# Modulation pieces of four k-tiles by 512 columns, and a ring of their own for the chunks that are not split

## The chip, the cores and the metric

The kernel runs on one core of a Trainium2 chip. The metric is the device time of one execution in microseconds (us); three runs of the kernel before are shown, and one execution was also profiled.

## What is computed

One layer of a hybrid diffusion backbone over 256 latent tokens and 256 context tokens with 2048 channels, in fp32. Cut to what matters here:

```python
mod_x = jnp.split((silu(c) @ w_ada + b_ada)[:, None, :], N_MOD, axis=-1)         # w_ada: 2048 x 12288, N_MOD = 6
mod_c = jnp.split((silu(c_ctx) @ w_ada + b_ada)[None, None, :], N_MOD, axis=-1)
hc = modulate(rmsnorm(ctx, norm1_w), mod_c[0], mod_c[1])    # modulate(h, shift, scale) = h * (1 + scale) + shift
hx = modulate(rmsnorm(x, norm1_w), mod_x[0], mod_x[1])
core_c, ctx_states = branch_core(hc, 1, p, None)            # h @ w_in, then the mixers
core_x, _ = branch_core(hx, rows, p, ctx_states)
x = x + mod_x[2] * branch_out(core_x, p)
hx2 = modulate(rmsnorm(x, norm2_w), mod_x[3], mod_x[4])
x = x + mod_x[5] * peer(hx2, ...)
```

The change is about the first two lines: two rows of activations (`c` and `c_ctx`) times the 96 MB matrix `w_ada`. Its first third (shift and scale of the first norm) is needed before anything else can be multiplied; the rest is needed late, from `mod_x[2]` on.

## The kernel before

**The stream of weights.** Weights reach the core as chunks of 128 x 1024 fp32 (512 KB). `Stream` (from line 33) holds a `plan`, the list of chunks in the order of their use. `ahead()` (line 58) issues loads through SP's queue up to `loads` = 7 chunks ahead of use (`_load`, line 39) and splits up to `splits` = 3 chunks ahead (`_split`, line 47). A split writes `hi`, the chunk rounded to fp32r, on ACT (line 52), and `lo = chunk - hi` on DVE (line 53); three fp32r matmuls (hi by hi, hi by lo, lo by hi) then stand for one fp32 product. The loaded chunks have a ring `raw` of 7 - 3 = 4 buffers, `hi` and `lo` of 4 each. Each `get()` takes the next chunk and calls `ahead()`.

**Modulation chunks are not split.** They stand in the same plan with a flag `False`, wait in the same raw ring (in the start two of three go to five more buffers, `raw0`, of the side pool `xp`), and are multiplied in fp32, which is two passes on PE. `ada_piece` (line 248) uses one chunk: four matmuls whose stationary side is `cS` (silu of `c` and `c_ctx`, two columns of 32 in use, line 244), each on a group of 32 columns of the array, side by side (`tile_position`), 256 columns each.

**Blocks.** `w_ada`'s first third (`w_ada0`) is 16 blocks of 4 chunks; a piece has four k-tiles by 256 columns. The rest (`w_ada1`, called `ride`) is 16 blocks of 8 chunks; a piece has two k-tiles by two 256-column halves. At the end of a block `ada_out` (line 256) copies the PSUM half bank `ad` to `adasb` on ACT (line 259), and two steps later PE transposes it in two pieces (line 264); DVE adds the four groups up (line 270) and adds `b_ada` (line 271) into `mods`.

**The start.** `START` (lines 139 to 150) is a list of steps, run by the loop in lines 369 to 402, and also sets the first part of the plan. In each of its first eight rounds come four chunks of block 8 + c (scale) and four of block c (shift), a step `h` (`h_pair`, line 296: two k-tiles of the normed and modulated input, `Hhi` and `Hlo`), and two each of the steps `v` (`v_part`, matmuls in lines 322 to 324) and `ld` (lines 393 to 395), from round 5 on also one chunk of k. Each piece also drives the generator `norm1` (line 279): per step four squares on ACT (line 284), three adds on DVE, a matmul with ones (line 287); then Ln and Exp (lines 289, 290), then eight multiplications of `xc` by the norm (line 293), two k-tiles each. The first `ahead()` stands at line 207, ahead of the constants (`ident` and on) and of all this.

**The units.** After the start come the projections as units (k, q, r, v, xs, ...); `mm3` (line 309, matmuls 314 to 316) does eight k-tiles of one chunk. `tick` (line 342) is called once per unit chunk, runs the waiting generators a step (`step`, line 333), and after every `RIDE` = 2 chunks lets `ride_piece` (line 349) do one modulation piece. 120 of the 128 ride that way, and `FILL` = 8 are done in a run near the second norm (loop near line 1122), from buffers of their own.

Of the kernel before, what the change touches and what calls it, by code (L numbers as in the profile page):

```python
# [10 lines left out]
F32 = mybir.dt.float32  # L11
F32R = mybir.dt.float32r
U32 = mybir.dt.uint32
# [15 lines left out]
class Stream:  # L29
# [3 lines left out]
    def __init__(self, nc, pool, loads, splits):  # L33
        self.nc, self.pool, self.loads, self.splits = nc, pool, loads, splits
        self.plan, self.raw, self.done = [], {}, {}
        self.cur = self.nd = self.ns = 0
        self.limit = self.side = None

    def _load(self, i):
# [4 lines left out]
        self.nc.sync.dma_start(t, self.plan[i][0])  # L44
        self.raw[i] = t

    def _split(self, i):
        t = self.raw.pop(i)
        if self.plan[i][1]:
            hi = self.pool.tile([P, 1024], F32R, name="hi", tag="hi", bufs=self.splits + 1)  # L50
            lo = self.pool.tile([P, 1024], F32R, name="lo", tag="lo", bufs=self.splits + 1)
            self.nc.scalar.activation(hi, t, AF.Copy)  # L52
            self.nc.vector.tensor_sub(lo, t, hi.bitcast(F32))  # L53
            self.done[i] = (hi, lo)
        else:
            self.done[i] = t
# [25 lines left out]
def hybrid_block_kernel(ctx, tc, A, out):  # L82
# [8 lines left out]
    st = Stream(nc, streams, 7, 3)  # L91
# [13 lines left out]
    def f_chunks(arr, f):  # L105
        return [(arr[f, h], True) for h in range(arr.shape[1])]
# [5 lines left out]
    RIDE, FILL = 2, 8  # L112
# [10 lines left out]
    def v_chunks(hd, q):  # L123
        return [(A["w_v"][hd, 2 * q + i], True) for i in range(2)]

    def unit_chunks(u):
        k, a, b = u
        first, n = {"k": (K0 + 2 * a + b, 1), "q": (Q0 + 2 * a, 2), "r": (R0 + 4 * a, 4), "xs": (X0 + 4 * a + b, 1),
                    "B": (B0 + a, 1), "C": (C0 + a, 1), "z": (Z0 + 4 * a + 2 * b, 2), "gl": (G0 + 2 * a, 2),
                    "v": (0, 0)}[k]  # L130
        if k == "v":
            return sum((v_chunks(a, q) for q in range(4)), [])
        if k == "k" and a < 2:
            return [(W[first, 1], True)]
        return sum((f_chunks(W, first + i) for i in range(n)), [])
# [16 lines left out]
    plan = []  # L152
    for k, a, b in START:
        if k == "ada":
            plan.append((A["w_ada0"][a, b], False))
        elif k == "v" and b == 0:
            plan.append((A["w_v"][0, a], True))
        elif k == "ld" and b == 0 and a % 2 == 0:
            plan.append((A["w_ld"][a // 2], True))
        elif k == "k":  # L160
            plan.append((W[K0 + a, 0], True))
    st.limit = len(plan)
    ride = [(A["w_ada1"][b, i], False) for b in range(16) for i in range(8)]
    nt = 0
    for u in units:
        for c in unit_chunks(u):
            plan.append(c)
            nt += 1
            if nt % RIDE == 0 and len(ride) > FILL:
                plan.append(ride.pop(0))  # L170
    assert len(ride) == FILL
# [6 lines left out]
    last_ada = ride  # L178
    QORD = [(j, e, h) for h in range(2) for j in range(2) for e in range(2)]
    QORD += [(j, e, h) for j in range(2, 8) for e in range(2) for h in range(2)]  # L180
    plan += [(A["w_q"][2 * j + e, h], True) for j, e, h in QORD]
    NB = 32
    for b in range(NB + BACK):
        for i in range(4):
            if b < NB:
                plan += f_chunks(A["u"], 4 * b + i)
            if b >= BACK:
                plan += [(A["v"][b - BACK, 2 * i + j], True) for j in range(2)]
# [3 lines left out]
    xpool = ctx.enter_context(tc.tile_pool(name="hpool", bufs=1))  # L192
# [13 lines left out]
    st.side = (xp, 5)  # L206
    st.ahead()
# [6 lines left out]
    ones512 = consts.tile([P, 256], F32, name="ones512")  # L214
    nc.vector.memset(ones512, 1.0)
# [7 lines left out]
    selF = consts.tile([P, 2, P], U32, name="selF")  # L223
    selB = consts.tile([P, 2, P], U32, name="selB")
    for n in range(2):
        nc.vector.tensor_scalar(selF[:, n], jp, 0.0, None, op0=OP.is_ge)
        nc.vector.tensor_scalar(selB[:, n], jp, 0.0, None, op0=OP.is_le)
# [20 lines left out]
    def ada_piece(i, ps, halves, raw=None):  # L248

        raw = (st.get() if raw is None else raw).rearrange("p (g n) -> p g n", g=4)  # L250
        nk = 4 // halves
        for g in range(4):
            mm_(ps[32 * g:32 * g + 32, :], cS[:, nk * i + g // halves, :], raw[:, g, :], start=i == 0, stop=i == KT // nk - 1,  # L253
                tile_position=(0, 32 * g), skip_group_check=True)

    def ada_out(b, ps, halves):

        sb = xpool.tile([P, 256], F32, name="adasb", tag="adasb", bufs=2)
        nc.scalar.activation(sb, ps, AF.Copy)
        yield  # L260
        yield
        p2 = scbank((P, 2, P))
        for t in range(2):
            nc.tensor.transpose(p2[:, t], sb[:, t * P:(t + 1) * P], ident)
        yield
        p2 = p2.rearrange("p t (j h m) -> p h t m j", h=halves, m=32)
        for h in range(halves):
            n = 2 * (halves * b + h)
            dst = mods[:, :, n:n + 2]
            nc.vector.tensor_reduce(dst.rearrange("p m t -> p t m"), p2[:, h, :, 0:2, :], axis=AX.X, op=OP.add)  # L270
            nc.vector.tensor_add(dst, dst, b_ada[:, None, n:n + 2].to_broadcast([P, 2, 2]))
        ended.add(("ada", b))
        yield
# [57 lines left out]
    ride_n, ride_ps = 0, None  # L331
# [17 lines left out]
    def ride_piece(raw=None):  # L349
        nonlocal ride_n, ride_ps  # L350
        b, i = divmod(ride_n, 8)
        if i == 0:
            ride_ps = adb[:, b % 2]
        ada_piece(i, ride_ps, 2, raw)
        if i == 7:
            bg.insert(0, ada_out(8 + b, ride_ps, 2))
        ride_n += 1
# [6 lines left out]
    adb = psum.tile([P, 2, 256], F32, name="ad")  # L364
    pv0 = [mmbank() for _ in range(4)]
    n1 = norm1()
    plr = pdt = None
# [36 lines left out]
    st.ahead()  # L404
    SZ = {"s1": 256, "s2": 512, "s4": 1024}
# [6 lines left out]

    lrS = wk.tile([P, 512], F32R, name="lrS")
# [29 lines left out]
    def decay(hd):  # L443
# [10 lines left out]
        def one(d, k):  # L454
# [12 lines left out]
            for n in range(2):  # L467
                s = slice(n * P, n * P + P) if d == 0 else slice(n * P + P - 1, n * P - 1 if n else None, -1)
                nc.vector.tensor_tensor_scan(B[:, k, s], ones512[:, :P], mn[:, s], 0.0, op0=OP.mult, op1=OP.add)
# [4 lines left out]
            nc.vector.tensor_tensor_scan(B[:, k, o], ones512[:, :255], mn[:, s], 0.0, op0=OP.mult, op1=OP.add)  # L474
# [152 lines left out]
    def dt_stage(pd):  # L627
# [26 lines left out]
        for c in range(4):  # L654
            s = slice(c * P, c * P + P)
            r = slice(c * P + P - 1, c * P - 1 if c else None, -1)
            nc.vector.tensor_tensor_scan(cum[rows[0], s], ones512[rows[0], :P], dA[rows[0], s], 0.0, op0=OP.mult, op1=OP.add)
            nc.vector.tensor_tensor_scan(cum[rows[1], r], ones512[rows[1], :P], dA[rows[1], r], 0.0, op0=OP.mult, op1=OP.add)
# [419 lines left out]
    def wo_load(i):  # L1078

        if i < 8:  # L1080
            nc.gpsimd.dma_start(x1[:, 2 * i:2 * i + 2], A["xc"][:, 2 * i:2 * i + 2, 0:256])
            if i < FILL:
                fill.append(x1p.tile([P, 1024], F32, name="fill", tag="fill", bufs=FILL))
                nc.gpsimd.dma_start(fill[-1], last_ada[i][0])
# [37 lines left out]
    for t in fill:  # L1122
        ride_piece(t)
# [183 lines left out]

    pq = {}
# [174 lines left out]
def _layouts(I):  # L1483
# [6 lines left out]
    L["w_ada0"] = f(w[:, :2 * D].reshape(4, 4, P, 16, 256).transpose(3, 0, 2, 1, 4)).reshape(16, 4, P, 1024)  # L1490
# [53 lines left out]
```

## Time and profile before

| | |
|---|---|
| time, median of three runs | 3682.08 us (3681.17 to 3683.45) |
| time of the profiled execution | 3680.64 us |
| its span on the core | 3678.8 us |
| granted TensorE clock, mean | 0.996 |
| PE matmuls, busy | 3619.1 us (98%), 24799 instructions |
| PE weight loads, busy | 3194.6 us (87%) |
| DVE, ACT, POOL busy | 61%, 45%, 10% |
| DMA | 715.51 MB, mean 194 GB/s |

The span is the time from the first to the last recorded instruction; 1.8 us of the execution lie around it. Busy times are of one profiled execution. Matmuls are pipelined and their ends are modelled, so that the distance between starts of matmuls tells more than their durations. A time in a timeline is counted from the start of the span. "Idle before" is the time in which an engine did nothing before an instruction, with the releaser, what ended it.

### The profile page before, as it was taken

How to read it: one execution, taken by the hardware profiler on the slowest of the kernel's cores; microseconds unless marked ns; L12 is line 12 of the kernel's file. 1: busy time of each engine (PE TensorE's matmuls, PEld its weight loads, DVE VectorE, ACT ScalarE, POOL GpSimd, SP SyncE). 2: the span in 40 equal slices, each digit the busy share in tenths (PEclk: the TensorE clock that was granted, in tenths of full speed). 3: DMA queues.
4: the chain of work that ended last, by engine and by line, in shares of the span. 5: the costliest groups of instructions: out<-in, count | busy, mean ns of one | idle time of the engine just before them, and what ended most of it. 6: DMA issues, size and time to landing. Idle time of an engine off the chain costs nothing.

```text
span 3678.8 us, 60850 instructions
## 1 busy us (share of the span) xinstructions
PE 3619.1 (98%) x24799; PEld 3194.6 (87%) x24799; DVE 2227.3 (61%) x3405; ACT 1669.3 (45%) x2248; POOL 370.1 (10%) x424
## 2 busy tenths in 40 slices
PE   6999999999999999999999999999999999999998
PEld 3688888888888888899999999999999999998886
DVE  4364443565566566656555788785555555556777
ACT  3244443344544455555444445554444444444444
POOL 0000000000000000011002006362000000000004
PEclk9999999999999999999999999999999999999999
DMA  8564444546555564467657556677665666666764
GB/s 341 214 177 142 151 166 164 188 152 199 192 172 164 185 204 144 135 206 266 195 189 258 176 179 197 200 200 228 197 198 196 199 197 198 196 199 202 244 227 141
DMA packets 196873, 715.51 MB, mean 194 GB/s; under 512 B 22769, under 2 KB 22913, under 8 KB 196081
## 3 DMA queue, kind: packets, MB, share of 16 engines
q1 hardware_dynamic: 171648, 625.03, 50.9%
q0 software_dynamic: 24944, 86.59, 8.5%
q8 instruction: 195, 3.19, 0.4%
q14 instruction: 86, 0.70, 0.1%
HBM read 679.93 MB, written 31.60 MB: 193 GB/s over the span
## 4 chain that ended last, share of the span: by engine, by line
PE 94%; DVE 2%; DMA 1%; ACT 1%; issue 1%; SPq 0%; POOL 0%; DVEq 0%; ACTq 0%; POOLq 0%
PE mm L314 20%; PE mm L315 20%; PE mm L316 20%; PE mm L1459 6%; PE mm L1460 6%; PE mm L1461 6%; PE ad L253 2%; PE mm L322 2%; PE sc L838 2%; PE mm L323 2%; PE mm L324 2%; PE sc L1267 2%; DVE lo L53 1%; PE sc L579 1%; PE sc L771 1%
## 5 line engine op out<-in xcount | busy, mean ns | idle before, releaser
L53 DVE TENSOR_TENSOR lo<-raw,hi 128x1024 fp32r<-128x1024 f32 x996 | 1235.1, 1247 | 1044.2 <-ACT hi L52 1040.4
L52 ACT ACTIVATE hi<-raw 128x1024 fp32r<-128x1024 f32 x996 | 1048.2, 1058 | 1248.8 <-PE mm L315 549.6
L314 PE MATMUL mm<-Hhi,hi 128*128 128x256 f32 (+1 forms) x2272 | 741.9, 327 | 3.7 <-ACT hi L52 3.1
L316 PE MATMUL mm<-Hhi,lo 128*128 128x256 f32 (+1 forms) x2272 | 723.0, 318 | 2.5 <-DVE lo L53 2.5
L315 PE MATMUL mm<-Hlo,hi 128*128 128x256 f32 (+1 forms) x2272 | 722.1, 318 | 0.0
L314 PE MATMUL mm<-h2hi,hi 128*128 128x256 f32 x2304 | 656.9, 285 | 3.3 <-ACT h2hi L1135 3.3
L315 PE MATMUL mm<-h2lo,hi 128*128 128x256 f32 x2304 | 652.4, 283 | 0.2
L316 PE MATMUL mm<-h2hi,lo 128*128 128x256 f32 x2304 | 651.8, 283 | 0.0
L314 PEld LDWEIGHTS mm<-Hhi,hi 128*128 128x128 f32 x2272 | 433.0, 191 | 82.3 <-issue 45.8
L316 PEld LDWEIGHTS mm<-Hhi,lo 128*128 128x128 f32 x2272 | 433.5, 191 | 33.0 <-DVE lo L53 3.1
L315 PEld LDWEIGHTS mm<-Hlo,hi 128*128 128x128 f32 x2272 | 433.7, 191 | 28.0 <-issue 0.5
L314 PEld LDWEIGHTS mm<-h2hi,hi 128*128 128x128 f32 x2304 | 441.6, 192 | 7.0 <-ACT h2hi L1135 3.7
L315 PEld LDWEIGHTS mm<-h2lo,hi 128*128 128x128 f32 x2304 | 441.9, 192 | 3.9 <-DVE h2lo L1138 0.7
L316 PEld LDWEIGHTS mm<-h2hi,lo 128*128 128x128 f32 x2304 | 441.6, 192 | 0.0
L1460 PE MATMUL mm<-lo,ph 128*128 128x512 f32 x1024 | 405.6, 396 | 4.5 <-DVE lo L53 4.5
L1459 PE MATMUL mm<-hi,ph 128*128 128x512 f32 x1024 | 406.3, 397 | 0.0
L1461 PE MATMUL mm<-hi,pl 128*128 128x512 f32 x1024 | 404.9, 395 | 0.0
L1460 PEld LDWEIGHTS mm<-lo,ph 128*128 128x128 f32 x1024 | 192.7, 188 | 48.6 <-DVE lo L53 6.0
L1461 PEld LDWEIGHTS mm<-hi,pl 128*128 128x128 f32 x1024 | 192.7, 188 | 46.6
L1459 PEld LDWEIGHTS mm<-hi,ph 128*128 128x128 f32 x1024 | 193.0, 188 | 43.1
L698 DVE SCALAR_TENSOR_TENSOR s<-mm,convw,s 128x189 f32<-128x189 f32 (+2 forms) x384 | 160.1, 427 | 111.5 <-ACT s L690 107.5
L316 PE MATMUL mm<-yh,lo 128*128 128x256 f32 x768 | 217.5, 283 | 1.3 <-DVE lo L53 1.3
(328 smaller groups left out, 4518.1 us busy)
## 6 DMA issues: line engine op xcount, KB each, us to landing
raw<-in_w_f_dram SPq DMA_DIRECT2D x288, 512.0 KB, 3.7
raw<-in_u_dram SPq DMA_DIRECT2D x256, 512.0 KB, 3.5
raw<-in_v_dram SPq DMA_DIRECT2D x256, 512.0 KB, 4.2
raw<-in_w_ada_dram SPq DMA_DIRECT2D x184, 512.0 KB, 4.3
raw<-in_w_so_dram SPq DMA_DIRECT2D x64, 512.0 KB, 3.4
raw<-in_w_v_dram SPq DMA_DIRECT2D x32, 512.0 KB, 3.9
s<-cum_d POOLq DMA_DIRECT2D x64, 256.0 KB, 6.6
raw<-in_w_ga_dram SPq DMA_DIRECT2D x32, 512.0 KB, 4.8
```

What stands on the lines that cost most here:

```text
L52: self.nc.scalar.activation(hi, t, AF.Copy)
L53: self.nc.vector.tensor_sub(lo, t, hi.bitcast(F32))
L253: mm_(ps[32 * g:32 * g + 32, :], cS[:, nk * i + g // halves, :], raw[:, g, :], start=i == 0, stop=i == KT // nk - 1, tile_position=(0, 32 ...
L314: mm_(ps, Whi[:, j, :], hi[:, k, tok], start=start and j == 0, stop=False)
L315: mm_(ps, Whi[:, j, :], lo[:, k, tok], start=False, stop=False)
L316: mm_(ps, Wlo[:, j, :], hi[:, k, tok], start=False, stop=stop and j == n - 1)
L322: mm_(pv[tb], Hhi[:, k, tok], Whi[:, j, :], start=k == 0, stop=False)
L323: mm_(pv[tb], Hhi[:, k, tok], Wlo[:, j, :], start=False, stop=False)
L698: nc.vector.scalar_tensor_tensor(dst, xi[:, r0 + dr:r1 + dr, c0 + dc:c1 + dc], w[:, t:t + 1], dst, op0=OP.mult, op1=OP.add)
L1459: mm_(ps[t, i], ghi, Whi, start=j == 0 and k == 0, stop=False)
L1460: mm_(ps[t, i], ghi, Wlo, start=False, stop=False)
L1461: mm_(ps[t, i], glo, Whi, start=False, stop=j == 1 and k == 1)
```

## The change

- The unsplit chunks leave the plan. They are a list of their own, `rides`, loaded in pairs by `board()` and taken by `alight()`. They have a ring `ride` of two buffers; in the start the five `raw0` of the side pool come on top, so that up to six chunks are aboard there (7 buffers), and two later. `board()` is called before the first `ahead()`, after each piece of the start, and in the units on the tick after a piece (`ticks % RIDE == 1`).
- The stream has 6 loads instead of 7, so its raw ring has 3 buffers. Its plan holds split chunks alone.
- A piece takes two chunks: four k-tiles by 512 columns, one k-tile per column group, into a whole bank `adb`. `w_ada0` is now 8 blocks of 4 pieces (each block has shift and scale of two k-tiles; its layout on the host follows), `w_ada1` 16 blocks of 4 pieces. In the start a piece stands on each odd step; `norm1` is driven two steps by each. `RIDE` is 4, `FILL` is 4.
- `ada_out` copies 512 columns into a buffer shared with others (`s4`, `s2`, `o2`), and instead of two transposes and a sum on DVE does four fp32 matmuls: stationary is a 128x128 part of the copy, moving is `sel2`, 128 x 2, which picks the two rows and adds the four groups. One addition on DVE with `b_ada` follows.
- `ones512`, `selF` and `selB` are replaced by broadcast views of `ones`, `maskF` and `maskB`.

```diff
     def _load(self, i):
-        if self.side and not self.plan[i][1] and i % 3:
-            t = self.side[0].tile([P, 1024], F32, name="raw0", tag="raw0", bufs=self.side[1])
-        else:
-            t = self.pool.tile([P, 1024], F32, name="raw", tag="raw", bufs=self.loads - self.splits)
...
+    def board(self):
+        while self.nr < len(self.rides) and len(self.aboard) + 2 <= 2 + (self.side[1] if self.side else 0):
+            for _ in range(2):
+                if self.side and self.nr % 7 > 1:
+                    t = self.side[0].tile([P, 1024], F32, name="raw0", tag="raw0", bufs=self.side[1])
+                else:
+                    t = self.pool.tile([P, 1024], F32, name="ride", tag="ride", bufs=2)
+                self.nc.sync.dma_start(t, self.rides[self.nr])
+                self.aboard.append(t)
+                self.nr += 1
...
-    st = Stream(nc, streams, 7, 3)
+    st = Stream(nc, streams, 6, 3)
...
-    RIDE, FILL = 2, 8
+    RIDE, FILL = 4, 4
...
-            if c < 8:
-                START.append(("ada", (8 + c, c)[i // 4], i % 4))
+            if c < 8 and i % 2:
+                START.append(("ada", c, i // 2))
...
     st.side = (xp, 5)
+    st.board()
     st.ahead()
...
+    sel2 = consts.tile([P, 2], F32, name="sel2")
+    nc.vector.tensor_reduce(sel2, ident.rearrange("p (j m) -> p m j", m=32)[:, 0:2, :], axis=AX.X, op=OP.add)
...
-        for g in range(4):
-            mm_(ps[32 * g:32 * g + 32, :], cS[:, nk * i + g // halves, :], raw[:, g, :], ...
+        raws = [r.rearrange("p (k n) -> p k n", k=2) for r in (raws or st.alight())]
+        for g in range(4):
+            mm_(adb[32 * g:32 * g + 32, :], cS[:, 4 * i + g, :], raws[g // 2][:, g % 2, :], ...
...
+    def ada_out(b):
+        sb = ada_sb()
+        nc.scalar.activation(sb, adb, AF.Copy)
+        yield
+        yield
+        p2 = scbank((P, 4, 2))
+        for t in range(4):
+            mm_(p2[:, t], sb[:, t * P:(t + 1) * P], sel2, start=True, stop=True)
+        yield
...
-        if riding and ticks % RIDE == 0 and ride_n < 128 - FILL:
+        if riding and ticks % RIDE == 0 and ride_n < 64 - FILL:
             ride_piece()
+        elif ticks % RIDE == 1:
+            st.board()
...
         if k == "ada":
-            if b == 0:
-                ps = adb[:, a // 8]
-            ada_piece(b, ps, 1)
+            ada_piece(b)
+            if st.nr < start_rides:
+                st.board()
             if b == 3:
-                bg.append(ada_out(a, ps, 1))
+                bg.append(ada_out(a))
+            next(n1, None)
             next(n1, None)
```

The lines move with it. In the changed kernel the split is in lines 49 (`hi`) and 50 (`lo`), a load of the stream in line 42, of `board` in line 61, the Silu of `cS` in line 247 and the squares of `norm1` in line 290.

The order of ACT's instructions at the head of the program, before (`sq` are the squares of `norm1`):

```order
L244 ACT_TABLE_LOAD [waits DMASW0_49]
L244 ACTIVATE cS<-cc 128x16x2 [waits DVE_49]
L245 ACT_TABLE_LOAD
L284 ACTIVATE sq_168<-xc 128x512 [waits DMAHW0_49]
L284 ACTIVATE sq_169<-xc 128x512
```

and in the changed kernel:

```order
L49 ACT_TABLE_LOAD
L49 ACTIVATE hi<-raw 128x1024 [waits DMAHW2_49]
L49 ACTIVATE hi<-raw 128x1024 [waits DMAHW3_49]
L49 ACTIVATE hi<-raw 128x1024 [waits DMAHW4_49]
L247 ACT_TABLE_LOAD [waits DMASW0_49]
L247 ACTIVATE cS<-cc 128x16x2 [waits DVE_49]
L248 ACT_TABLE_LOAD
L290 ACTIVATE sq_183<-xc 128x512 [waits DMAHW0_49]
```

Three splits, each behind its own transfer, now stand ahead of `cS` and of the first square; DVE's three `lo` (line 50) stand in the same way ahead of `ident` and the other constants.

The order of SP's loads in the changed kernel, in the block of the start that holds the second chunk of w_v (`ride` and numbered `raw` are modulation chunks; `raw<-in_w_ld` is a split chunk of the stream's ring):

```order
L61 DMA ride<-in_w_ada_dram 128x1024 [waits DMAHW0_49,PE_49]
L61 DMA ride<-in_w_ada_dram 128x1024 [waits DMAHW1_49,PE_49]
L42 DMA raw<-in_w_ld_dram 128x1024 [waits DMAHW2_49,DVE_49]
L61 DMA raw_429<-in_w_ada_dram 128x1024 [waits DMAHW3_49,PE_49]
L61 DMA raw_431<-in_w_ada_dram 128x1024 [waits DMAHW4_49,PE_49]
L61 DMA raw_461<-in_w_ada_dram 128x1024 [waits DMAHW5_49,PE_49]
```

The load of w_ld waits for DVE, which has to read an older chunk out of that ring, and the modulation chunks behind it wait only for PE; with one queue they go in this order.

## Rows read from the trace of the kernel before

**Rows 1.** The page, part 4: the chain that ended last, by engine.

```profile
PE 94%; DVE 2%; DMA 1%; ACT 1%; issue 1%; SPq 0%; POOL 0%; DVEq 0%; ACTq 0%; POOLq 0%
```

**Rows 2.** Timeline, PE: start us, us, engine line op out<-in xcount [idle before].

```profile
46.74 0.79 PE L322 MATMUL mm<-hi,Hhi 128*128 128x512 f32 x1
...
62.34 0.64 PE L253 MATMUL ad<-raw,cS 128*32 128x256 f32 x8 [0.56 <-ACT adasb L259]
...
74.13 1.93 PE L253 MATMUL ad<-raw,cS 128*32 128x256 f32 x32
76.63 0.64 PE L253 MATMUL ad<-raw,cS 128*32 128x256 f32 x8 [0.56 <-ACT adasb L259]
...
175.55 0.50 PE L314 MATMUL mm<-Hhi,hi 128*128 128x512 f32 x1 [0.50 <-ACT s L440]
```

**Rows 3.** Timeline of all engines, 602.4 to 604.2 us.

```profile
602.57 0.28 PE L316 MATMUL mm<-Hhi,lo 128*128 128x256 f32 x1
...
602.77 0.16 PEld L253 LDWEIGHTS ad<-raw,cS 128*32 128x32 f32 x8
602.78 0.64 PE L253 MATMUL ad<-raw,cS 128*32 128x256 f32 x8
...
603.34 0.19 PEld L314 LDWEIGHTS mm<-Hhi,hi 128*128 128x128 f32 x1 [0.41 <-issue]
603.35 0.50 PE L314 MATMUL mm<-Hhi,hi 128*128 128x512 f32 x1
603.45 0.19 PEld L315 LDWEIGHTS mm<-Hlo,hi 128*128 128x128 f32 x1
...
603.68 0.39 PE L315 MATMUL mm<-Hlo,hi 128*128 128x512 f32 x1
```

**Rows 4.** The chain that ended last, in order of time: start us, us, line.

```profile
757.78 3.43 PE sc L771 x8
```

**Rows 5.** Timeline, PE, 262.4 to 263.8 us.

```profile
262.87 0.28 PE L316 MATMUL mm<-Hhi,lo 128*128 128x256 f32 x1
262.99 0.38 PE L264 MATMUL sc<-ident,adasb 128*128 128x128 f32 x2
...
263.33 0.28 PE L315 MATMUL mm<-Hlo,hi 128*128 128x256 f32 x1
```

**Rows 6.** Tile adasb: xcount, ns min/median/max, first and last start, forms.

```profile
L259 ACT ACTIVATE adasb<-ad x32: 360/383/385, 28.5 to 2056.0; 128x256 f32<-128x256 f32 x32
```

**Rows 7.** The chain that ended last, its start.

```profile
2.78 14.50 DMA raw<-in_w_ada_dram
```

**Rows 8.** DMA view, 0 to 60 us in 40 slices of 1.5 us.

```profile
GB/s 0 197 410 410 420 384 388 383 187 274 401 404 415 410 410 410 404 415 410 172 0 30 333 388 410 418 418 393 412 415 410 407 412 407 404 407 273 279 93 11
```

**Rows 9.** The page, part 5: busy us, mean ns, idle before and releaser.

```profile
L53 DVE TENSOR_TENSOR lo<-raw,hi 128x1024 fp32r<-128x1024 f32 x996 | 1235.1, 1247 | 1044.2 <-ACT hi L52 1040.4
L52 ACT ACTIVATE hi<-raw 128x1024 fp32r<-128x1024 f32 x996 | 1048.2, 1058 | 1248.8 <-PE mm L315 549.6
```

**Rows 10.** Timeline, DVE, 0 to 62 us.

```profile
2.34 0.23 DVE L211 TENSOR_SCALAR ident<-jp 128x128 f32<-128x128 f32 x1 [2.34 <-POOL jp L209]
...
3.91 0.48 DVE L243 MEMSET cS<- 128x512 f32 x1
...
32.03 3.50 DVE L293 TENSOR_TENSOR xc<-xc,rs 128x1024 f32<-128x1024 f32 x3 [2.68 <-ACT rs L290]
```

**Rows 11.** Timeline, ACT, 0 to 62 us.

```profile
8.27 0.23 ACT L244 ACTIVATE cS<-cc 128x32 f32<-128x32 f32 x1
...
9.81 1.15 ACT L284 ACTIVATE sq<-xc 128x512 f32<-128x512 f32 x2
...
20.54 1.15 ACT L284 ACTIVATE sq<-xc 128x512 f32<-128x512 f32 x2 [2.64 <-PE sc L287]
...
31.36 0.63 ACT L290 ACTIVATE rs<-rs 128x512 f32<-128x512 f32 x1
```

**Rows 12.** Tile raw, 0 to 40 us: from issue to landing.

```profile
DMA to landing us min/median/max: 3.4/8.3/16.9
```

More of the change, by code (lines that the diff above doesn't have):

```diff
@@ L37, in __init__ @@
         self.limit = self.side = None
+        self.rides, self.aboard, self.nr = [], deque(), 0
     def _load(self, i):
-        if self.side and not self.plan[i][1] and i % 3:
-            t = self.side[0].tile([P, 1024], F32, name="raw0", tag="raw0", bufs=self.side[1])
-        else:
-            t = self.pool.tile([P, 1024], F32, name="raw", tag="raw", bufs=self.loads - self.splits)
-        self.nc.sync.dma_start(t, self.plan[i][0])
+        t = self.pool.tile([P, 1024], F32, name="raw", tag="raw", bufs=self.loads - self.splits)
+        self.nc.sync.dma_start(t, self.plan[i])
         self.raw[i] = t
@@ L48, in _split, with alight @@
         t = self.raw.pop(i)
[L49 to L56, printed above, removed]
+        hi = self.pool.tile([P, 1024], F32R, name="hi", tag="hi", bufs=self.splits + 1)
+        lo = self.pool.tile([P, 1024], F32R, name="lo", tag="lo", bufs=self.splits + 1)
+        self.nc.scalar.activation(hi, t, AF.Copy)
+        self.nc.vector.tensor_sub(lo, t, hi.bitcast(F32))
+        self.done[i] = (hi, lo)
+    def board(self):
[8 more added lines that the diff above has]
+                self.nr += 1
+    def alight(self):
+        return [self.aboard.popleft() for _ in range(2)]
     def ahead(self):
@@ L105, in f_chunks @@
     def f_chunks(arr, f):
-        return [(arr[f, h], True) for h in range(arr.shape[1])]
+        return [arr[f, h] for h in range(arr.shape[1])]
     W = A["w_f"]
     Q0, K0, R0, Z0, X0, B0, C0, G0 = 0, 8, 16, 32, 64, 96, 104, 112
-    RIDE, FILL = 2, 8
+    RIDE, FILL = 4, 4
     units = [("k", 0, 0), ("k", 0, 1), ("q", 0, 0)]
@@ L123, in v_chunks @@
     def v_chunks(hd, q):
-        return [(A["w_v"][hd, 2 * q + i], True) for i in range(2)]
+        return [A["w_v"][hd, 2 * q + i] for i in range(2)]
     def unit_chunks(u):
@@ L154, in hybrid_block_kernel @@
         if k == "ada":
-            plan.append((A["w_ada0"][a, b], False))
+            st.rides += [A["w_ada0"][a, 2 * b + i] for i in range(2)]
         elif k == "v" and b == 0:
-            plan.append((A["w_v"][0, a], True))
+            plan.append(A["w_v"][0, a])
         elif k == "ld" and b == 0 and a % 2 == 0:
-            plan.append((A["w_ld"][a // 2], True))
+            plan.append(A["w_ld"][a // 2])
         elif k == "k":
-            plan.append((W[K0 + a, 0], True))
+            plan.append(W[K0 + a, 0])
     st.limit = len(plan)
-    ride = [(A["w_ada1"][b, i], False) for b in range(16) for i in range(8)]
-    nt = 0
+    ride = [A["w_ada1"][b, i] for b in range(16) for i in range(8)]
+    start_rides = len(st.rides)
+    st.rides += ride[:-2 * FILL]
     for u in units:
[L166 to L171, printed above, removed]
+        plan += unit_chunks(u)
+    assert len(plan) - st.limit >= RIDE * (64 - FILL)
     for f in range(16):
@@ L177, in hybrid_block_kernel @@
         plan += f_chunks(A["w_o"], f)
-    last_ada = ride
+    last_ada = ride[-2 * FILL:]
     QORD = [(j, e, h) for h in range(2) for j in range(2) for e in range(2)]
     QORD += [(j, e, h) for j in range(2, 8) for e in range(2) for h in range(2)]
-    plan += [(A["w_q"][2 * j + e, h], True) for j, e, h in QORD]
+    plan += [A["w_q"][2 * j + e, h] for j, e, h in QORD]
     NB = 32
@@ L187, in hybrid_block_kernel @@
             if b >= BACK:
-                plan += [(A["v"][b - BACK, 2 * i + j], True) for j in range(2)]
+                plan += [A["v"][b - BACK, 2 * i + j] for j in range(2)]
     st.plan = plan
-    xpool = ctx.enter_context(tc.tile_pool(name="hpool", bufs=1))
     es_h = ExitStack()
@@ L222, in hybrid_block_kernel @@
     nc.vector.tensor_scalar(maskB, jp, 0.0, None, op0=OP.is_le)
[L223 to L227, printed above, removed]
+    selF, selB = (m.bitcast(U32)[:, None, :].to_broadcast([P, 2, P]) for m in (maskF, maskB))
     b_ada = cload("b_ada", [P, 96])
@@ L345, in tick, with ride_piece @@
         ticks += 1
-        if riding and ticks % RIDE == 0 and ride_n < 128 - FILL:
+        if riding and ticks % RIDE == 0 and ride_n < 64 - FILL:
             ride_piece()
[L349 to L356, printed above, removed]
+        elif ticks % RIDE == 1:
+            st.board()
+    def ride_piece(raws=None):
+        nonlocal ride_n
+        b, i = divmod(ride_n, 4)
+        ada_piece(i, raws)
+        if i == 3:
+            bg.insert(0, ada_out(8 + b))
         ride_n += 1
@@ L404, in hybrid_block_kernel @@
     st.ahead()
+    st.board()
     SZ = {"s1": 256, "s2": 512, "s4": 1024}
@@ L468, in one @@
                 s = slice(n * P, n * P + P) if d == 0 else slice(n * P + P - 1, n * P - 1 if n else None, -1)
-                nc.vector.tensor_tensor_scan(B[:, k, s], ones512[:, :P], mn[:, s], 0.0, op0=OP.mult, op1=OP.add)
+                nc.vector.tensor_tensor_scan(B[:, k, s], ones, mn[:, s], 0.0, op0=OP.mult, op1=OP.add)
             if d == 0:
@@ L1121, in hybrid_block_kernel @@
     stats(*prev)
-    for t in fill:
-        ride_piece(t)
+    for i in range(FILL):
+        ride_piece(fill[2 * i:2 * i + 2])
     rs2 = x1p.tile([P, 256], F32, name="rs2")
```

51 lines of the change are left out of this document (23 added, 28 removed).

## The prediction

> **What bounds the kernel now.** I read the page first: the chain that ended last is 94% TensorE (PE) [rows 1], so a microsecond of PE work added or removed is a microsecond of the kernel, and other work counts only where PE waits for it. The places where PE waits are next. In the timeline of PE's first 176 us the loop over `START` makes its first real matmul (`v_part`) at 46.74 and hands over to the units at 175.55 [rows 2]; after that PE's timeline has almost no idle time beside the ride pieces. So three things are to be priced: a ride piece, the end of a modulation block (`ada_out`), and the way to 46.74.
>
> **Ride pieces.** An isolated piece stands between two ordinary matmuls: from 602.57 to 603.68 are 1.11 us, of which 0.12 and 0.23 are the ordinary steps of the 256- and 512-column matmuls, so the piece costs 0.76 [rows 3]. In a run of pieces the eight passes of four come in 1.93 us less the 0.40 of the last one itself, seven steps of 0.22, so a piece is 0.43 [rows 2]. The other 0.33 is paid for entering and leaving the column-tiled work, once per visit. A piece of four k-tiles by 512 columns has the same two passes, each twice as long: an fp32 pass of 512 columns takes 0.43 (3.43 for eight) [rows 4], so 0.86 + 0.33 = 1.19, against 2 x 0.76 = 1.52 for the two pieces it replaces. The 120 pieces that ride on units become 60: **60 x 0.33 = -20 us**. All of it is on PE's path. The four last pieces (`fill`) stay a run in a place where PE then waits for the second norm: nothing; if that cover went, 0.33 at most, as the columns are the same.
>
> **Ends of blocks.** Before, two transposes per block: from 262.87 to 263.33 are 0.46, less two steps of 0.12: 0.22 [rows 5]. There are 32 blocks [rows 6], 7 us in all. Now there are 24 blocks with four true fp32 matmuls each, whose weights are the 128x128 block itself and whose moving side is `sel2` with two columns. Each is two passes with a weight load of its own, eight loads a block. No row shows a matmul of two columns. Below: four transposes, 0.44. Above: each 128-column load in full, 8 x 0.19 = 1.52 [rows 3]. I take the distance at which two 128-column loads start when no streaming holds the second up, 603.34 to 603.45, so 8 x 0.11 plus one load with no matmul over it, **0.95**. It is the only row with two such loads back to back. That adds 0.73 a block; the 15 riding blocks and the last one make **+11.7 us**, the eight of the start are counted below. The Trainium skill's page "TensorE: Matmul & The Clock Gate", section "Back-to-back issue gap", allows a matmul of 1 to 64 columns about 25 ns; a block would by an estimate from it be 0.2 us, and the sum 18 us lower. The row of the two loads speaks against that, and no run here yet shows two columns; it is rival 1.
>
> **The way to the first real matmul.** This is the part that the diff hides. Before, the plan began with modulation chunks, which are not split, so the first `ahead()` put no work on ACT and DVE. Now the plan holds split chunks alone, and the same call, still ahead of the constants and `norm1`, puts three splits at the head of both queues (the order of ACT above). They wait for w_v, w_ld, w_v, which SP issues behind xc and six ride chunks. The first 512 KB chunk landed at 2.78 + 14.50 = 17.28 [rows 7]; at 410 GB/s [rows 8] each next one takes 1.28 us, so the seventh to ninth land at 24.96, 26.24 and 27.52. ACT's last split (1.06) ends at 28.6, DVE's (1.25, queued one behind the other) at about 29.9 [rows 9]. Behind them on DVE stand the constants up to the memset of cS: 2.34 to 4.39 before [rows 10], some 0.55 less now, so 31.4. Then cS (0.23) and a table load: the squares start 1.54 after cS does [rows 11], at 32.9 instead of 9.81, **23.1 us late**. The squares lose their 2.64 of waiting for PE, since both sums on PE now follow one piece; the last two sums may run at the half pace of the early rows, +0.9. rs1 was ready at 31.36 + 0.63 = 31.99 [rows 11], so now at about 53.4. All eight multiplications of xc (3.50 for three) [rows 10] stand before the first h_pair on DVE: 9.35, to 62.8. Modulation add, s1, two tensor_scalars and one Hhi take 1.8 more: the first v matmul at **64.6 instead of 46.74, +17.9**. The pieces of blocks 0 and 1 are done by about 62 in the shadow of this, as their number is the same; if they were not, they would add their lateness.
>
> **The rest of the start.** A block was 14.29 us, 62.34 to 76.63 [rows 2]; 36 matmuls at 0.23 leave 6.0 for modulation, 0.56 of that PE's wait for ACT at the block's first piece. Now: two isolated pieces, a run of two (0.33 + 4 x 0.43) and one end, 2 x 1.19 + 2.05 + 0.95 = 5.4. That saves 0.6 in the three plain blocks and about 1 in the three with a k chunk (one more isolated piece before): **-4.8**. Against it stands SP. In the block of the second v chunk, SP holds the load of a w_ld chunk ahead of the pair for the block's last piece (the order of SP above). That load waits for DVE's lo of a chunk whose hi has to wait until PE ends this v chunk: 2.5 us after that end at the earliest. A transfer needs at least 3.4 to land [rows 12], and the pair lands 1.28 and 2.56 behind it, 8.5 after the end of v. PE is there 3.75 after it and needs the second half 0.5 later: some 4.3 of new idle time; two milder cases of 0.3 to 0.6 bring it to **+5**. The start as a whole: 17.9 - 4.8 + 5 = **+18**, bounds +11 (no stall on SP, ends of blocks at 0.44) and +26 (stalls in each block).
>
> **What I put at nothing.** Loads 7 to 6 and the raw ring 4 to 3: a load is used for its split three chunks after it is issued, at least 8.6 us (24 x 0.12 x 3), against 3.4 to land; if the cover goes, ACT stands still first and PE only three chunks later. Fewer DVE operations per block, a wider ACT copy, the shared buffers (s4, s2, o2) and the broadcast masks run beside PE. The split of three real chunks ahead instead of about two makes ACT wait for PE more often in the riding stretch; PE's own work covers it.
>
> **The sum**, against the profiled execution (span 3678.8, time 3680.64): +18 - 20 + 11.7 = +9.7, and I take +9.5: 3690.1. The median of the three runs shown is 1.4 above that execution, so **3691.5 us**.
>
> **Rivals.**
> 1. *The ends of blocks are cheap* (the other side). If loads of so short matmuls overlap as the 32-column ones do, eight of which start within 0.16 - 0.11 = 0.05 us [rows 3], a block's end costs 0.1 to 0.2 instead of 0.95: -0.8 x 24 = -19, 3672, faster. At the price of four transposes (0.44) it is -12, 3679, the same. It decides below 0.55 a block; from there on the kernel is not slower. For it: matmuls have no columns to wait for. Against it: those loads go to different columns of the array, these to the same.
> 2. *The loads are not overlapped at all*: 1.52 a block, +0.57 x 24 = +14, 3705. Against it: loads overlap matmuls all over the trace.
> 3. *The ride ring starves PE.* On the units `board()` holds one pair only, and its loads stand behind a load that waits for DVE's lo. The pair has four chunks of time (at least 11.5 us) and needs about 2.5 + 0.8 + 3.4 + 2.6 = 9.3. DVE would have to be late by 2 us and more; if 15 of the 60 pieces then wait for one transfer of 1.28, +19, 3711. For it: the busy stretches of conv and ssd; against it: no ride piece waited for its load there before.
> 4. *The wider piece does not work as one.* Its second half waits for a second chunk; if its two column groups then start only after the first two are through, a piece costs 0.33 + 4 x 0.43 = 2.05, nothing is gained and 60 x 0.86 = +51 comes on top, 3743. Against it: in the runs of before each piece has a wait of its own, and the passes still come at 0.22.
>
> **How the numbers follow.** Forecast 0.62, rival 1 0.15 (0.05 at the low end, 0.10 near the transposes), rival 2 0.10, rival 3 0.10, rival 4 0.03. A measurement of this kernel tells about 0.2% from no change, 7.4 us: 3674.7 to 3689.4 is the same. The forecast's own spread, 3682 to 3701, comes from the bounds of the start; of its 0.62 about 0.37 lies above 3689.4 and 0.25 below. Slower 0.37 + 0.10 + 0.10 + 0.03 = 0.60, same 0.25 + 0.10 = 0.35, faster 0.05. The range 3678 to 3705 leaves out the low end of rival 1 and most of rivals 3 and 4.
>
> **What would show it.** Right: the first square at about 33, the first v matmul at 63 to 66, the units from about 194, isolated pieces at 1.19, block ends near 0.95, an idle stretch of about 4 us before a piece in the second v block. Wrong: squares before 20 (then the splits do not block ACT), block ends under 0.55 or over 1.3, pieces on the units that wait for w_ada transfers, or a stretch behind the start that differs by more than the 8 us of pieces and ends.

## The result, and the profile after

The changed kernel took 3707.41 us, the median of four runs (3703.47 to 3709.48), against 3681.62 us before (four runs, 3681.15 to 3683.45): a ratio of 1.0068 with a 95% interval of 1.0050 to 1.0085. It is **slower by 26 us**. Forecast were 3691.5 us and a range of 3678 to 3705; the sign was right and the size was not.

The span grew from 3678.8 to 3705.9 us. Where, is seen from the starts of the same matmuls in both traces:

| stage | before, from | after, from | difference there | added in the stage | forecast for it |
|---|---|---|---|---|---|
| first v matmul | 46.74 | 63.58 | +16.8 | +16.8 | +17.9 |
| units | 175.55 | 199.95 | +24.4 | +7.6 | about 0 |
| first chunk of w_ga | 1665.77 | 1680.85 | +15.1 | -9.3 | -9 |
| first chunk of w_o | 1944.12 | 1958.68 | +14.6 | -0.5 | 0 |
| end of the span | 3678.8 | 3705.9 | +27.1 | +12.5 | +0.7 |

So three of five rows came as forecast (the third with some luck, see below), and two did not: the rest of the start, and the stretch from w_o on. The chain that ended last names the newcomer, DMA with 3% where it had 1% [rows 1]:

```profile
PE 92%; DMA 3%; DVE 2%; issue 1%; ACT 1%; SPq 0%; DVEq 0%; POOL 0%; ACTq 0%; POOLq 0%
```

**What came as forecast.** First the way to the first v matmul, in ACT's timeline of the changed kernel (columns as in [rows 2]):

```profile
24.78 1.06 ACT L49 ACTIVATE hi<-raw 128x1024 fp32r<-128x1024 f32 x1 [22.78 <-DMA raw<-in_w_v_dram]
...
28.31 1.28 ACT L247 ACT_TABLE_LOAD   x1
30.89 0.23 ACT L247 ACTIVATE cS<-cc 128x32 f32<-128x32 f32 x1 [1.29 <-DVE cS L246]
...
32.43 1.15 ACT L290 ACTIVATE sq<-xc 128x512 f32<-128x512 f32 x2
```

and in DVE's:

```profile
25.87 3.68 DVE L50 TENSOR_TENSOR lo<-raw,hi 128x1024 fp32r<-128x1024 f32 x3 [25.87 <-ACT hi L49]
29.47 0.22 DVE L218 TENSOR_SCALAR ident<-jp 128x128 f32<-128x128 f32 x1
...
52.24 9.17 DVE L299 TENSOR_TENSOR xc<-xc,rs 128x1024 f32<-128x1024 f32 x8 [2.68 <-ACT rs L296]
```

ACT does nothing until w_v's first chunk lands; the constants on DVE stand behind the three `lo`. The first square starts at 32.43 (forecast 32.9, before 9.81 in [rows 11]), the first v matmul at 63.58 (forecast 64.6).

Then a piece and the end of a block, in PE's timeline:

```profile
63.58 0.50 PE L328 MATMUL mm<-hi,Hhi 128*128 128x512 f32 x1
...
609.15 0.28 PE L322 MATMUL mm<-Hhi,lo 128*128 128x256 f32 x1
609.36 1.07 PE L257 MATMUL ad<-ride,cS 128*32 128x512 f32 x8
...
610.58 0.28 PE L321 MATMUL mm<-Hlo,hi 128*128 128x256 f32 x1
...
856.75 0.28 PE L322 MATMUL mm<-Hhi,lo 128*128 128x256 f32 x1
856.87 0.95 PE L268 MATMUL sc<-sel,s 128*128 128x2 f32 x8
...
857.89 0.28 PE L321 MATMUL mm<-Hlo,hi 128*128 128x256 f32 x1
```

From 609.15 to 610.58 are 1.43, less two ordinary steps of 0.12: the piece costs 1.19, as forecast. From 856.75 to 857.89 are 1.14, less 0.24: the end of a block costs 0.90 (forecast 0.95).

**What did not.** The largest waits of PE (total us, times, longest):

```profile
PE ad L257 <- ACT cS L247: 31.2, 1, 31.2
PE mm L322 <- DVE lo L50: 8.6, 9, 1.6
PE sc L293 <- DVE sq L292: 8.6, 4, 4.0
PE ad L257 <- DMA raw<-in_w_ada_dram: 6.5, 4, 3.6
PE sc L692 <- DVE s L681: 5.0, 1, 5.0
PE mm L1470 <- DVE lo L50: 4.5, 2, 3.9
PE sc L1108 <- ACT x1q L1126: 3.8, 1, 3.8
```

The row with `lo` L50 and L322 stood at 3.8 us in 5 times before, and its nine times now lie from 1674 us on, seven of them in the w_o stretch (6.9 us). The last row is the end of that stretch; it stood at 1.1. The row with w_ada's transfers is the start. The granted clock beside it (column PEclk; columns: stretch, us, busy time and instructions of PE, PEld, DVE, ACT, POOL, then PEclk, DMA share, GB/s):

```profile
76.00:84.00 8.00, 6.85 (x38) 3.20 (x30) 2.14 (x5) 1.75 (x3) 0.00 (x0) 1.00 0.96 345
84.00:88.30 4.30, 4.30 (x15) 3.44 (x15) 0.00 (x0) 0.00 (x0) 0.00 (x0) 0.60 0.53 214
88.30:93.70 5.40, 5.40 (x31) 2.59 (x29) 2.27 (x6) 1.09 (x2) 0.00 (x0) 1.00 0.06 10
93.70:99.60 5.90, 1.25 (x8) 0.14 (x4) 1.92 (x4) 1.23 (x2) 0.00 (x0) 0.89 0.96 361
99.60:105.40 5.80, 5.75 (x14) 3.28 (x15) 1.23 (x1) 1.54 (x2) 0.00 (x0) 0.52 1.02 418
```

PE stood still for 1.10 us before 82.36, for 3.64 before 97.47 and for 1.07 before 99.65. Behind each idle stretch it then ran most of some 5 us at the lower of its two levels (1.2 GHz, not 2.4): mean granted clock 0.60 over 4.3 us and 0.52 over 5.8 us, a loss of 0.40 x 4.3 + 0.48 x 5.8 = 4.5 us that no row of waits shows. The idle time, too, is less than what was lost: in the piece before 84 us,

```profile
80.21 1.05 PE L257 MATMUL ad<-raw,cS 128*32 128x512 f32 x4
82.36 1.05 PE L257 MATMUL ad<-raw,cS 128*32 128x512 f32 x4 [1.10 <-DMA raw<-in_w_ada_dram]
```

the first half starts 2.15 us before the second, whose chunk comes late. The profile counts 1.05 of this as busy; where both chunks are there, the halves run side by side (eight matmuls in 1.07 at 609.36). And while PE used up what had landed, from 88.3 to 93.7, the transfers moved 10 GB/s.

### The profile page after: what moved, and what is told of

Read it like the earlier page. It is cut to its first block, busy times and chain, and to the rows that moved or that the text cites. A ratio compares the mean times of both kernels' runs of the same rounds, so it can differ in the third digit from the quotient of the medians.

```text
span 3705.9 us, 59536 instructions
## 1 busy us (share of the span) xinstructions
PE 3620.5 (98%) x24159; PEld 3192.5 (86%) x24159; DVE 2212.7 (60%) x3329; ACT 1676.2 (45%) x2241; POOL 370.7 (10%) x424
## 4 chain that ended last, share of the span: by engine, by line
PE 92%; DMA 3%; DVE 2%; issue 1%; ACT 1%; SPq 0%; DVEq 0%; POOL 0%; ACTq 0%; POOLq 0%
PE mm L320 20%; PE mm L321 19%; PE mm L322 19%; PE mm L1470 6%; PE mm L1469 6%; PE mm L1471 6%; PE ad L257 2%; PE sc L847 2%; PE mm L328 2%; PE sc L1276 2%; PE mm L329 1%; PE mm L330 1%; DVE lo L50 1%; DMA ride<-in_w_ada_dram 1%; PE sc L588 1%
## 5 line engine op out<-in xcount | busy, mean ns | idle before, releaser
L50 DVE TENSOR_TENSOR lo<-raw,hi 128x1024 fp32r<-128x1024 f32 x996 | 1233.3, 1244 | 1253.8 <-ACT hi L49 1239.6
L322 PE MATMUL mm<-Hhi,lo 128*128 128x256 f32 (+1 forms) x2272 | 721.3, 317 | 0.9 <-DVE lo L50 0.9
L322 PE MATMUL mm<-h2hi,lo 128*128 128x256 f32 x2304 | 651.7, 283 | 0.0
L322 PEld LDWEIGHTS mm<-Hhi,lo 128*128 128x128 f32 x2272 | 432.3, 190 | 30.6 <-DVE lo L50 1.2
L322 PEld LDWEIGHTS mm<-h2hi,lo 128*128 128x128 f32 x2304 | 441.6, 192 | 0.0
L320 PE MATMUL mm<-yh,hi 128*128 128x256 f32 x768 | 217.6, 283 | 0.9 <-ACT hi L49 0.9
L322 PE MATMUL mm<-yh,lo 128*128 128x256 f32 x768 | 217.7, 283 | 0.8 <-DVE lo L50 0.8
```

The costliest lines, as they stand in the source:

```text
L320: mm_(ps, Whi[:, j, :], hi[:, k, tok], start=start and j == 0, stop=False)
L322: mm_(ps, Wlo[:, j, :], hi[:, k, tok], start=False, stop=stop and j == n - 1)
```

## The experiments

Theory: four separate costs, all on PE's path. (a) The splits at the heads of the queues, 16.8 us; (b) SP, which holds back modulation chunks behind a load of the stream, with the slow clock after it, about 10; (c) the raw ring of three buffers in the w_o stretch, 12.2; (d) the ends of blocks, 24 x (0.90 - 0.44). The first four kernels take away one each; times are compared with the changed kernel's 3707.41. The kernel before took 3681.62 us beside the changed kernel and 3683.11 beside these four, so that such a difference is good to some 1.5 us.

### Splits behind the first h_pair

```diff
-    def ahead(self):
+    def ahead(self, splits=True):
...
-        while self.nd < min(n, self.cur + self.loads):
+        while self.nd < min(n, self.cur + self.loads - (0 if splits else self.splits)):
...
-        while self.ns < min(n, self.cur + self.splits):
+        while splits and self.ns < min(n, self.cur + self.splits):
...
     st.board()
-    st.ahead()
+    st.ahead(False)
...
             h_pair(a)
+            if a == 0:
+                st.ahead()
```

> The changed kernel with one thing moved: the first three splits are recorded behind the first h_pair instead of ahead of the constants (and only three stream chunks are loaded until then). Theory (the splits at the heads of ACT's and DVE's queues cost the 16.8 us between the first v matmul of the changed kernel, 63.58, and of the one before, 46.74): first square at about 10 us, first v matmul at 45 to 48, units from 183 to 188 instead of 199.95, the time 12 to 17 us below the changed kernel. Rival (the first stretch is bound by the transfers of xc and the modulation chunks, some 410 GB/s, whatever stands in the queues): first v matmul earlier, but waits for w_ada chunks take its place and the units still begin at 195 or later.

Measured: 3692.77 us (nine runs), 14.6 below; the first square at 9.80, the first v matmul at 47.62, the units from 186.37. PE's rows:

```profile
17.84 3.04 PE L257 MATMUL ad<-ride,cS 128*32 128x512 f32 x8 [17.84 <-DMA ride<-in_w_ada_dram]
...
47.62 0.49 PE L328 MATMUL mm<-hi,Hhi 128*128 128x512 f32 x1 [1.27 <-ACT hi L49]
```

The theory holds for the first stretch: PE's first work waits for its own transfer and no longer for `cS`. Of the 16.0 us won there 13.6 are left at the units. The stalls of (b) remain, as in the changed kernel; new waits of PE behind the late splits (0.8 us for `lo`, 0.7 for a ride chunk) are 1.5 of the 2.4 lost again, and the rest is not accounted for.

### A ring of five behind the units

```diff
-        t = self.pool.tile([P, 1024], F32, name="raw", tag="raw", bufs=self.loads - self.splits)
+        if i >= self.late and i % 5 in (1, 3):
+            t = self.pool.tile([P, 1024], F32, name="ride", tag="ride", bufs=2)
+        else:
+            t = self.pool.tile([P, 1024], F32, name="raw", tag="raw", bufs=3)
...
-        while self.nd < min(n, self.cur + self.loads):
+        while self.nd < min(n, self.cur + self.loads + 2 * (self.nd >= self.late)):
```

(`late` is the place in the plan of the first w_ga chunk, rounded up to a multiple of 5.)

> The changed kernel with one thing added: behind the units, when nothing rides any more, the two buffers of the ride ring join the stream's ring (five buffers, eight loads ahead). Theory (from w_o to the first w_q chunk the changed kernel loses 12.3 us, because three raw buffers do not cover the 4 us that DVE waits for the store of x1 in each pass): these 12.3 us go to about 0, ACT no longer waits for w_o transfers, time 10 to 13 us below the changed kernel. Rival (the loss comes from the queue of POOL or from the wider pieces of fill): at most 3 us.

Measured: 3696.26 us (five runs), 11.1 below. What is lost against the kernel before between the first chunks of w_o and the fifth of w_q falls from 12.2 to 2.1 us (9.7 of the 12.2 lie ahead of the first w_q chunk); up to w_o the two kernels run alike within 1.2 us. What happens in one pass over w_o in the changed kernel (all engines but PE, 1995 to 2008 us):

```profile
1997.29 1.06 ACT L49 ACTIVATE hi<-raw 128x1024 fp32r<-128x1024 f32 x1 [5.24 <-DMA raw<-in_w_o_dram]
...
2000.69 0.56 POOL L1122 DMA_DIRECT2D x_d<-x  x1 [9.62 <-DVE x L1120]
...
2004.36 0.62 DVE L1128 TENSOR_SCALAR x<-x,sc 128x256 f32<-128x256 f32 x2 [3.96 <-DMA x_d<-x]
2004.89 3.49 DVE L50 TENSOR_TENSOR lo<-raw,hi 128x1024 fp32r<-128x1024 f32 x3
```

DVE scales x1 in place and has to wait 3.96 us until the store of x1 has read it. Three `lo` stand behind that, and three raw buffers are what the ring has: until these `lo` have run, SP can start no load, and ACT then waits for one (5.24 us in the first row, which ends the wait of the pass before). The kernel before had the same wait on DVE (1950 to 2050 us),

```profile
DVE x L1119 <- DMA x_d<-x: 35.5, 7, 5.8
```

about as long as in the changed kernel (1968 to 2075 us),

```profile
DVE x L1128 <- DMA x_d<-x: 31.9, 8, 4.7
```

but four buffers. In the waits of ACT over this stretch, the changed kernel (1976 to 2088 us),

```profile
ACT hi L49 <- DMA raw<-in_w_o_dram: 34.6, 12, 5.3
```

the kernel before (1960 to 2047 us),

```profile
ACT hi L52 <- PE mm L315: 25.4, 19, 1.8
```

and the kernel with five buffers (1968 to 2077 us):

```profile
ACT hi L52 <- PE mm L325: 27.6, 15, 2.2
```

With four or five buffers ACT is ahead and waits for PE; with three it waits for memory. PE's seven waits for `lo` in the w_o stretch (6.9 us) are one of 0.2 with five buffers, and the sum of x1q waits 1.1 us again, as before. The edit gives buffers and loads ahead together, so the two are not told apart. The rival (POOL's queue, the wider pieces of `fill`) is left with some 2 us.

### Modulation chunks of the start through POOL's queue

```diff
-                self.nc.sync.dma_start(t, self.rides[self.nr])
+                (self.nc.gpsimd if self.side and self.nr > 5 else self.nc.sync).dma_start(t, self.rides[self.nr])
```

> The changed kernel with the modulation chunks of the start, from the seventh on, issued by POOL's queue instead of SP's. Theory (SP stands in front of loads of the stream that wait for DVE, and holds back modulation chunks that could be loaded): the idle stretches of PE before pieces at 82.4, 97.5 and 99.7 (5.8 us) go, and with them the stretches at half clock behind them (about 4.5 us); units from 188 to 193 instead of 199.95, time 7 to 11 us lower. Rival (the transfers themselves are the limit): the idle stretches stay, units at 198 to 202.

Measured: 3695.25 us (six runs), 12.2 below, a little more than expected; units from 188.40. Waits for w_ada's `raw` chunks are 0.7 us in all, and the same stretch of the start has the full clock:

```profile
76.00:90.00 14.00, 14.00 (x79) 8.42 (x79) 4.61 (x10) 2.81 (x4) 4.47 (x9) 1.00 0.91 350
90.00:105.00 15.00, 15.00 (x85) 8.73 (x87) 6.66 (x14) 3.75 (x5) 4.96 (x10) 1.00 0.93 354
```

The transfers run on at 350 GB/s where they had fallen to 10. So it was the order in SP's one queue, not the transfers: the way from the first v matmul to the units went from 136.4 to 122.7 us. Matmul by matmul against this kernel, the changed one loses 2.2 us at the piece of 80.21, 1.7 at the lower clock behind it, 6.9 at the pieces up to 101.5 (with the waits before 97.47 and 99.65), 1.6 behind them and 1.2 at the piece of 119.86, where the profile shows no idle time of PE, as the first half runs meanwhile: 13.6 in all, where idle time (5.8) and slow clock (4.5) make 10.3.

### Ends of blocks by transposes

```diff
-        p2 = scbank((P, 4, 2))
+        p4 = scbank((P, 4, P))
         for t in range(4):
-            mm_(p2[:, t], sb[:, t * P:(t + 1) * P], sel2, start=True, stop=True)
+            nc.tensor.transpose(p4[:, t], sb[:, t * P:(t + 1) * P], ident)
         yield
+        p2 = sum2.tile([P, 4, 2], F32, name="sum2", tag="sum2", bufs=2)
+        nc.vector.tensor_reduce(p2, p4.rearrange("p t (j m) -> p t m j", m=32)[:, :, 0:2, :], axis=AX.X, op=OP.add)
```

> The changed kernel with the ends of blocks as before: four transposes by ident and a sum on DVE instead of four matmuls with sel2. Theory (each end costs 0.90 us of PE with sel2, because eight 128-column weight loads follow each other, and 0.22 per two transposes): an end costs 0.44, 24 ends save 0.46 each, 9 to 11 us in all. Rival (ends in the start are hidden by waits, and DVE's sum delays the next step): only the 15 riding ends count, 5 to 7 us.

Measured: 3697.62 us (six runs), 9.8 below. An end is now, in PE's timeline of this kernel,

```profile
850.09 0.28 PE L325 MATMUL mm<-Hhi,lo 128*128 128x256 f32 x1
850.21 0.60 PE L269 MATMUL sc<-ident,s 128*128 128x128 f32 x4
...
850.77 0.28 PE L324 MATMUL mm<-Hlo,hi 128*128 128x256 f32 x1
```

0.68 less 0.24, so 0.44: four transposes with 64 times as many columns cost half of four fp32 matmuls with two. The units begin 3.9 us earlier; the eight ends of the start at 0.46 are 3.7, so they seem to count as well, but this execution also had the full clock from 84 to 88.3, where the changed kernel had 0.60.

### All four, and the splits ahead

> The changed kernel with the four edits together: splits behind the first h_pair, modulation chunks of the start through POOL's queue, the ring of five behind the units, ends of blocks by transposes. Theory (four separate costs, each on PE's path): the gains add up, 14.6 + 12.2 + 11.1 + 9.8 = 47.7 below 3707.4, so 3660; where the gains of the start overlap, up to 3668; in both cases below the kernel before by 14 us and more. Rival (the start is then bound by the 44 MB of transfers at some 410 GB/s, 107 us, and by DVE's norm): first v matmul still near 46 but units at 180 or later, 3672 and more.

Measured: **3659.68 us** (five runs, 3659.56 to 3664.48), ratio to the kernel before 0.9937 (0.9924 to 0.9951). The four gains add up to 47.7 us, and 47.7 were measured between the medians. That the two agree to the tenth is luck: with each time set against the kernel before that ran beside it, the four gains add up to 53.7 and the four edits together give 49.3. So the costs add up within some 4 us. This version beats both kernels; the first v matmul is at 49.17 and the units begin at 172.76, which is earlier than before.

One large wait was left, PE's 5.0 us for DVE's chain that prepares dt, near 240 us in the changed kernel and before 213.7 in this one. The next kernel tries its cause alone:

```diff
-        while self.ns < min(n, self.cur + self.splits):
+        while self.ns < min(n, self.cur + self.splits - (self.limit is None and self.ns < self.late)):
```

> The changed kernel with one thing changed: while the units run, only two chunks are split ahead instead of three (loads and rings as they are). Theory (DVE's lo stands behind ACT's hi of a chunk that has to wait for PE to free a hi buffer, so the chain that prepares dt on DVE starts 2.6 us later after the units' begin than before, and PE waits 5.0 instead of 1.2 us for it near 240): the wait near 240 falls to 1 to 3 us, the time is 2 to 4 us lower. Rival (three splits ahead are needed to cover busy stretches of ACT and DVE in the units): the wait goes, but new waits of PE for lo or hi take its place, time the same or up to 5 us higher.

Measured: 3728.3 us (four runs), 21 us **above** the changed kernel. The wait did fall, but the expected gain did not come; of the rival only the sign was right, since the new waits are not for hi and lo. PE's waits from 190 to 1420 us:

```profile
PE ad L258 <- DMA ride<-in_w_ada_dram: 15.6, 11, 3.1
PE sc L693 <- DVE s L682: 2.4, 1, 2.4
```

In the changed kernel the same two rows are:

```profile
PE sc L692 <- DVE s L681: 5.0, 1, 5.0
PE ad L257 <- DMA ride<-in_w_ada_dram: 2.0, 2, 1.7
```

This is the third rival of the prediction, the pair of modulation chunks that comes too late on the units. With six loads and two splits ahead, a load wants the buffer of a chunk whose split is recorded only when PE takes the next chunk; SP stands there, and the pair stands behind it. The same kernel with all four edits:

> All four edits and two splits ahead in the units. Theory: what the two-split kernel gains against the changed one comes on top of the four, 2 to 4 us below the kernel with the four edits. Rival: the same time as that kernel or up to 5 us above it.

Measured: 3686.95 us (eleven runs), 27 above the kernel with four edits, so that both the theory and the rival failed: the loss is not tied to the start or to w_o. Two kernels tell the cause. One issues the pairs of the units through POOL's queue, too (`if self.nr > 5` alone in the line above); one leaves them on SP and takes five loads ahead instead of six:

```diff
-        while self.nd < min(n, self.cur + self.loads + 2 * (self.nd >= self.late) - ...
+        while self.nd < min(n, self.cur + self.loads + (2 if self.nd >= self.late else -(self.limit is None)) - ...
```

> The kernel with four edits and two splits ahead, and the modulation chunks of the units, too, issued by POOL's queue. Theory (with two splits the load six ahead stands on SP until the next chunk is taken, and the pairs of modulation chunks stand behind it; that alone made PE wait for ride transfers): these waits, 39.0 us in 12 times there with 18.4 of them the first landing, fall to about 19, and the time to 3655 to 3660. Rival (POOL has waits of its own in the units that hold the pairs back, or the pairs are late because of the transfers themselves): the waits stay at 30 us and more and the time at 3675 to 3690.

> The kernel with four edits and two splits ahead, and in the units five loads ahead instead of six, so that a load never waits for a split that is not yet recorded; all loads of the units on SP. Theory (the same as for the run with POOL's queue): the waits for ride transfers fall from 39.0 to about 19 and the wait for dt near 240 stays at 2 to 3 us; time 3655 to 3660. Rival (five loads ahead are too few: ACT waits for transfers and PE behind it): waits of PE for hi and lo in the units, 3665 or more.

Measured: 3665.30 us with POOL's queue and 3662.65 us with five loads (five runs each; ratios to the kernel before 0.9954, 0.9941 to 0.9968, and 0.9951, 0.9937 to 0.9964). The waits fell as the theory has it; the times are 3 to 5 us above the 3655 to 3660 expected. PE's waits for pairs from 165 to 1420 us, with six loads on SP,

```profile
PE ad L262 <- DMA ride<-in_w_ada_dram: 20.0, 9, 5.8
```

with POOL's queue,

```profile
PE ad L262 <- DMA ride<-in_w_ada_dram: 3.0, 1, 3.0
```

and with five loads:

```profile
PE sc L701 <- DVE s L690: 2.4, 1, 2.4
PE ad L262 <- DMA ride<-in_w_ada_dram: 2.1, 1, 2.1
```

Either edit takes most of the waits away, so the pairs were late because of what stood ahead of them in SP's queue. Late on the units the kernel with five loads stands 4.7 us ahead of the one with four edits, by their traces; in time the two can't be told apart (their intervals overlap), and the 3659.68 of the simpler one is the lowest median.

## Why the prediction was right and wrong

- **Ride pieces**: right. 1.19 us each; at these prices 60 x 0.33 = 20 us were won. Rival 4 fell (2.05 a piece); halves one after the other are seen only where the second chunk came late.
- **Ends of blocks**: right in mechanism and nearly in size, 0.90 for 0.95. The words for the 0.95, eight distances of 0.11 plus one load, make 1.07 with the 0.19 of a load, so that part of its nearness is luck. Rival 1 fell: at 0.90 the end lies well above its 0.55; so did rival 2 (1.52). The Trainium skill's page "TensorE: Matmul & The Clock Gate" lists about 25 ns for a matmul of so few columns in "Back-to-back issue gap", by an estimate from it 0.2 us a block; that was not seen here. An end with eight weight loads costs 0.90 and one with four 0.44, 0.11 a load in both, with 2 columns as with 128: the weight loads set the price.
- **The way to the first v matmul**: right, +16.8 for +17.9, and the run with late splits shows that it is the queues' heads.
- **The rest of the start**: wrong by 7. The step "two milder cases of 0.3 to 0.6 bring it to +5" had the mechanism, SP's queue, and the idle time of the main stall (4.7 measured before the two halves of that block's last piece, for 4.3), but the term measured +13.6. It counted idle time alone and left out PE's clock after a stall (4.5 us) and the first half of a piece, which runs alone while the second waits; the "milder cases" cost 2.2 and 1.2 us. The saving of 4.8 came out as 6.1 (128.8 us from the first v matmul to the units before, 122.7 with the chunks through POOL's queue), but 2.0 of that are the clock again: the kernel before ran from 46.74 to 50.74 at 0.50.
- **"What I put at nothing": loads 7 to 6 and the raw ring 4 to 3**: wrong by 12.2 us, the largest error. It was worked out from PE's pace and a landing time of 3.4 us, for the case that a buffer is given back as soon as its chunk is due for a split. In w_o it is given back when DVE comes to it, and DVE stood for 4 us per pass behind a store. The condition "if the cover goes" was stated, and the case was not priced. The prediction's last sign of being wrong, a stretch behind the start that differs by more than 8 us, is this one.
- **"The split of three real chunks ahead ... PE's own work covers it"**: wrong by 3.8 us, the wait near 240 us (5.0 for 1.2). With two splits ahead it is 2.4; so the number of splits has a part in it. Why DVE's chain then still ends 2.4 late, against 1.2 before, was not tried.
- **Rival 3** did not decide here (2.0 us of waits). With two splits ahead it came true, at 21 us for its 19; the waits were 11 with 15.6 us in all, not 15 of 1.28.

In the sum: 16.8 + 7.6 in the start, -20 for pieces, 15 x 0.68 = +10.2 for the ends that ride, +3.8 at 240 us, +12.2 in w_o make 30.6; the spans differ by 27.1, so there are some 3.5 us of small gains, 3.3 of them on the units (-9.3 for -6.0). There PE's waits for hi and lo fell from 5.6 to 2.0 us and those for w_ada rose from nothing to 2.0, a gain of 1.6; the rest is not accounted for. So the units came as forecast (-9.3 for -9) in part by luck: the wait near 240 was not in the forecast, and these gains were not either.

## What to carry to other kernels

When a ring of buffers gets smaller, find in the trace the longest wait of the engine that gives its buffers back, in every stage that uses the ring, and not only the mean pace: the ring has to cover that wait. Loads with different reasons to wait shouldn't share one in-order queue, and a load shouldn't be issued ahead of the point where the split that frees its buffer is recorded. The head of each engine's program is a place of its own: whatever is recorded first there holds back everything behind it until its first transfer lands.

## What the runs showed of the hardware that was not expected

- A stall of PE can cost more than its length: in the changed kernel the granted clock behind idle stretches of 1 to 4 us was 0.60 and 0.52 for 4 to 6 us, and the distance between 512-column matmuls 0.43 us instead of 0.23. With the stalls gone it was 1.00 in the same stretch. It does not follow each time: the kernel with the ring of five has the same start, and behind an idle stretch of 0.85 us before 82.72 its clock stayed at 1.00 (columns as above):

```profile
84.00:88.30 4.30, 4.30 (x23) 3.69 (x23) 0.00 (x0) 0.00 (x0) 0.00 (x0) 1.00 0.62 255
```

- Four fp32 matmuls of two columns cost 0.90 us, twice as much as four transposes of 128 columns (0.44). The former need eight weight loads of 0.19 us, which at 0.90 for eight come 0.11 apart; the latter need four of 0.14, as far apart. All loads of the 23 ends up to 1420 us (duration in ns, min/median/max), in the changed kernel and in the one with transposes:

```profile
L268 PEld LDWEIGHTS sc<-sel,s x184: 186/192/192, 57.4 to 1420.5; 128*128 128x128 f32 x184
```

```profile
L269 PEld LDWEIGHTS sc<-ident,s x92: 137/140/144, 58.4 to 1410.1; 128*128 128x128 f32 x92
```
